# A decoder layer on one core: the mixer's first projection runs ahead of its norm, four residuals one by one, and another pace for the adaLN columns

## The chip, the cores and the metric

The kernel runs on one core of one Trainium2 chip. A core has TensorE (matrix products, PE in the profile, with its weight loads as PEld), VectorE (DVE), ScalarE (ACT), GpSimd (POOL) and SyncE (SP), which here issues the transfers. Each engine works through its own list of instructions in order; semaphores between the lists make one wait for another. The metric is the device time of one execution in microseconds; lower is better.

## The reference

One layer, batch 1, T = 256 tokens, D = 2048, all in float32:

```
mod = silu(c) @ ada_w + ada_b          # 9 vectors of 2048: sh1 sc1 gt1 sh2 sc2 gt2 sh3 sc3 gt3
h = rmsnorm(x) * g1 * (1 + sc1) + sh1
x = x + 0.5 * gt1 * ((silu(h @ wg1) * (h @ wu1)) @ wd1)        # SwiGLU_1, inner width 5632
h = rmsnorm(x) * g2 * (1 + sc2) + sh2
x = x + gt2 * (mixer(h) @ w_out)                               # 8 FoX heads, 8 GatedDeltaNet heads
h = rmsnorm(x) * g3 * (1 + sc3) + sh3
x = x + 0.5 * gt3 * ((silu(h @ wg2) * (h @ wu2)) @ wd2)        # SwiGLU_2
out = rmsnorm(x) * final_norm
```

The mixer projects h onto queries, keys and values of both groups of heads, onto 24 gate columns (forget gate, decay, beta) and onto z. The delta-rule heads put a causal convolution of 4 taps and a SiLU behind their projections, and work in chunks of 64 tokens; the FoX heads do softmax attention with a forgetting term.

## The kernel before, in words

**Layout.** Activations stand transposed: x is 16 tiles of 128 features by 256 tokens. All weights come as one stream of 5392 tiles of 128x128, 8 to a block of 512 KB, 674 blocks in the order of use. A product of float32 values is made from three products of a high part and a low part. So each block is loaded (raw, L124), ACT writes its high part whi (L127), DVE the rest wlo = wraw - whi (L139), and TensorE does three times 256 columns per tile, or 512 and 256 columns where one instruction takes both parts of the activation. Raw, whi and wlo have four buffers each: DVE and ACT can be up to four blocks ahead of TensorE, and a block's wlo has to be there before the third product of its first tile. h is kept as high and low part in hs.

**Stages and blocks.** SwiGLU_1 takes blocks 0 to 263. Its first 28 inner tiles come first (gate and up products to block 111, in pieces over k because the first norm's shift and scale come in bit by bit; partial sums are added up by DVE in acc, L587), then the down product to 167, then 16 inner tiles (gate, up to 231, down to 263). The mixer has 264 to 409: a first projection with four sums at once (24 gate columns and the keys of GatedDeltaNet heads 0 to 2; 64 tiles, 264 to 271), further projections one by one, and the output projection from 378 on: first four columns at once (378 to 385), then 12 columns one by one, two blocks each. SwiGLU_2 has the rest.

**adaLN columns.** mod has 144 columns of 128 values. A column is a transfer of 1 MB (L260) and one reduction of 128x2048 on DVE (L264). The table RATE says, by block, how many columns are issued per block: ada_col is called from Stream.next when the sum passes one. ada_need issues on the spot what is missing.

**Residual and norm.** When a down column is done, residual adds both halves of its sum to x (L516, L517), and sumsq_add squares it on ACT and adds it up on GpSimd (L313, L317). Ahead of the mixer, modulate waits for the last column: norm_sums adds over the features with TensorE (nsum), ACT and DVE make the inverse root, norm_row spreads it over a row with TensorE (nrow), and only then modulate_one writes hs[j] (DVE, ACT, DVE for each of 16 tiles). h_need keeps it four tiles ahead of the products. Ahead of SwiGLU_2 there is another way, class Early: y writes x*g unnormed into hs as soon as a column of x is there, the products start on that, step puts nsum at k = 2 and nrow at k = 4 between them and from then on lets modulate_one overwrite the hs tiles already used, and scaled multiplies the sums by the row afterwards. The shift rides along as two more columns of the moving tile (258 for 256).

**Order.** The program is written once, and a scheduler then orders each engine's list by its own estimates. Inside the mixer, tick counts time along the projections; the generators gates, decays, keys, solve, gdn, fox and to_out are advanced when their last yielded gap has passed. The output projection calls after for the first four columns together, right behind their products; for later columns it waits in the list owed, until tile 8 (LATER) of the next column.

Of the kernel before, what the change touches and what calls it, by code (L numbers as in the profile page):

```python
# [8 lines left out]
F32 = mybir.dt.float32  # L9
# [7 lines left out]
P = 128  # L17
# [10 lines left out]
NH = 8  # L28
# [7 lines left out]
RATE = ((0, 0.5), (12, 0.45), (68, 0.06), (112, 0.5), (168, 0.38), (264, 0.0), (284, 0.26), (404, 0.0), (424, 0.125))  # L36
# [7 lines left out]
LATER = 8  # L44
BEHIND = 2
# [108 lines left out]
def layer_kernel(ctx: ExitStack, tc: tile.TileContext, xrow, c, adaw, cols, cst, w, out, order, dbg=None):  # L154
# [204 lines left out]
    plain = hsf[:, : KD * HS].rearrange("p (k i) -> p k i", k=KD)[:, :, : 2 * T].rearrange("p k (q t) -> p k q t", q=2)  # L359

# [7 lines left out]
    def modulate_one(j, g1, sh, r, weave=True):  # L368

        t = pt("ht")  # L370
        hl, hh, tt = (run(j, LO), run(j, HI), turns(t)) if weave else (plain[:, j, LO], plain[:, j, HI], t)
# [20 lines left out]
    def modulate(which, m_sh, m_sc):  # L392
        ada_need(max(m_sh, m_sc), KD - 1)
        g1 = gains(which, m_sc, 0, KD)
        r = norm_row(norm_sums())
        hq["next"], hq["one"] = 0, lambda j: modulate_one(
            j, g1[:, j : j + 1], mod[:, m_sh * KD + j : m_sh * KD + j + 1], r, False)

    class Early:
# [3 lines left out]
        def __init__(self, which, m_sh, m_sc):  # L403
            self.which, self.m_sh, self.m_sc, self.row, self.rstd = which, m_sh, m_sc, None, None

        def y(self, j):
# [8 lines left out]
            A.activation(run(j, HI), turns(x[:, j]), AF.Copy, scale=g)  # L415
            V.scalar_tensor_tensor(run(j, LO), turns(x[:, j]), g, run(j, HI).bitcast(F32), ALU.mult, ALU.subtract)

        def step(self, k):
# [3 lines left out]
            if k == 4:  # L422
                self.row = norm_row(self.rstd, A.copy)
                g1 = gains(self.which, self.m_sc, 0, KD)
                hq["next"], hq["one"] = 0, lambda j: modulate_one(
                    j, g1[:, j : j + 1], mod[:, self.m_sh * KD + j : self.m_sh * KD + j + 1], self.row)
# [8 lines left out]
        def scaled(self, dst, ps):  # L435
# [4 lines left out]
            V.tensor_tensor(dst, ps[:, :T], self.row, ALU.mult)  # L440
# [308 lines left out]
    norm2 = Early(2, 6, 7)  # L749
# [5 lines left out]
    def mixer():  # L755
        modulate(1, 3, 4)
# [29 lines left out]
        def project(items):  # L786

            pp = [psn(i, "pp") for i in range(len(items))]
            todo = [(i, k) for k in range(KD) for i in range(len(items))]
            for i, k in todo:  # L790
                m, n = items[i]
                h_need(k)
                wh, wl = W.next(m, k, n)
                hh, hl = woven(plain[:, k, HI]), woven(plain[:, k, LO])
# [3 lines left out]
                tick(TILE_US)  # L798
            return [p_[:, :T] for p_ in pp]

        def project_rows(mat, grp):

            pv = [psb("pv0"), psb("pv1")]
            for k in range(KD):
                wh, wl = W.next(mat, k, 4 * grp, 4)
                for t in range(2):
                    hh, hl = (plain[:, k, q, t * P : (t + 1) * P] for q in (HI, LO))
# [17 lines left out]
        def gates(ps):  # L825

            yr = x[:, 8]
            A.copy(runs(yr[R]), turns(ps[R]))
# [93 lines left out]
        def decays(half):  # L922
# [9 lines left out]
            yield 1.0  # L932
# [8 lines left out]
        def conv_silu(ps, n, dst):  # L941
# [4 lines left out]
            for s in range(1, 4):  # L946
                V.scalar_tensor_tensor(cv[:, s:], cp[:, : T - s], tap(3 - s), cv[:, s:], ALU.mult, ALU.add)
# [221 lines left out]
        def fox(h, qk, vt):  # L1169
# [5 lines left out]
            yield 1.0  # L1175
# [14 lines left out]
            yield 3.0  # L1190
# [5 lines left out]
            yield 1.0  # L1196
# [15 lines left out]
            yield 5.0  # L1212
# [8 lines left out]
        def have_keys(h, ps):  # L1221
            kk[h] = otile("kk")
            conv_silu(ps, NH + h, kk[h].bitcast(F32)[:, 0])
# [49 lines left out]
        first = project([("gt", 0)] + [("qkv", NH + h) for h in range(3)])  # L1273
        start("k", -1, gates(first[0]))
        for h in range(3):
            have_keys(h, first[1 + h])
# [6 lines left out]
        for js in [list(range(4))] + [[j] for j in range(4, KD)]:  # L1283

            j = js[0]
            one_ = psf if j < 6 or j >= KD - 2 else pss if j < 8 else psb
            pj = [psn(i, "po") for i in range(len(js))] if len(js) > 1 else [one_("po")]
            if js[0] in BACK:
                x_back(1 + BACK.index(js[0]))
            for i, k in enumerate(ko):  # L1290
# [4 lines left out]
                if owed and i == LATER:  # L1295
                    owed.pop(0)()
# [4 lines left out]
            def after(js=js, pj=pj):  # L1301
# [169 lines left out]
```

## Time and profile before

Three runs: median 1944.64 us, 1944.19 to 1946.02. The profiled execution took 1944.91 us; its span, on which all later times count from zero, is 1943.1 us.

| stretch of the span, us | what runs | PE busy, us | DVE busy, us | granted clock |
|---|---|---|---|---|
| 20.00 to 170.00 | SwiGLU_1, first gate and up pieces | 140.90 of 150.00 | 139.97 | 1.00 |
| 170.00 to 330.00 | its later pieces | 160.00 of 160.00 | 135.65 | 0.99 |
| 330.00 to 483.00 | first down product | 150.90 of 153.00 | 144.28 | 1.00 |
| 483.00 to 740.40 | second gate, up and down | 256.79 of 257.40 | 234.39 | 1.00 |
| 740.40 to 746.60 | to the mixer's first product | 2.29 of 6.20 | 5.50 | 0.70 |
| 769.60 to 1167.00 | mixer behind its first projection | 387.83 of 397.40 | 335.80 | 1.00 |
| 1167.00 to 1184.00 | output projection, around column 5 | 14.30 of 17.00 | 15.80 | 0.90 |
| 1240.00 to 1943.00 | SwiGLU_2 and the end | 694.80 of 703.00 | 461.23 | 1.00 |

How to read it: an engine's row counts time in which at least one of its instructions is under way, so neighbours that overlap by a little (DVE starts the next 128x1024 subtraction 1.13 us after one that took 1.22 us) fill the time without a gap. The clock is the share of full speed that the throttle granted to TensorE. A row of the timeline has start, time from the first start to the last end, engine, line, operation, tiles, count and, in brackets, the idle time of the engine before it and what ended it.

### The profile page before, as it was taken

Reading aid. Unit: us, or ns where it says so; the run is one execution under the profiler, and the core shown is the slowest. Engines: PE = TensorE matmul, PEld = TensorE weight load, DVE = VectorE, ACT = ScalarE, POOL = GpSimd, SP = SyncE. Lnnn points to the kernel's source line nnn. Section 1 sums busy time; section 2 is a strip of 40 time slices with the busy share of each in tenths; the row PEclk is TensorE's granted clock in tenths of the full one; section 3 lists DMA queues with packets and bytes.
Section 4 is the critical chain, followed back from the end, with each engine's and each line's share of the span. In section 5 each row is a group of like instructions: output and inputs, shape, how many; then the busy total and the mean of one; then the engine's idle time right before and its main releaser. Section 6 shows DMA issues by size and latency. Waiting matters only on the chain.

```text
span 1943.1 us, 33703 instructions
## 1 busy us (share of the span) xinstructions
PE 1903.0 (98%) x13086; PEld 1774.5 (91%) x13087; DVE 1555.1 (80%) x2414; ACT 1039.5 (53%) x1647; POOL 57.4 (3%) x55
## 2 busy tenths in 40 slices
PE   8999999999999999999999999999999999999998
PEld 7999999988999988889989998999999999999997
DVE  6999888989999997789987989877676765666654
ACT  7433555433455446857757655665554445555553
POOL 0000000000000020000000002100000000000011
PEclk9999999999999999999999999999999999999999
DMA  9998867999989985596567567677777766666663
GB/s 374 350 344 345 294 215 265 400 374 376 361 347 348 349 307 211 197 330 219 204 254 250 207 229 281 206 246 264 240 246 262 244 231 199 203 199 202 200 201 120
DMA packets 129490, 519.58 MB, mean 267 GB/s; under 512 B 18217, under 2 KB 21545, under 8 KB 111153
## 3 DMA queue, kind: packets, MB, share of 16 engines
q1 hardware_dynamic: 129330, 517.42, 74.1%
q8 instruction: 103, 1.69, 0.3%
q14 instruction: 57, 0.47, 0.1%
HBM read 512.89 MB, written 4.47 MB: 266 GB/s over the span
## 4 chain that ended last, share of the span: by engine, by line
PE 77%; DVE 12%; issue 4%; ACT 3%; DMA 2%; SPq 0%; DVEq 0%; ACTq 0%
PE pd L492 12%; PE pu L488 10%; PE pg L488 10%; PE pd L493 6%; PE pu L489 5%; PE pg L489 5%; DVE wlo L139 5%; PE pgu L574 4%; PE pgu L572 4%; PE pgu L573 4%; DVE adat L264 3%; PE po L492 2%; PE pp L795 2%; PE pp L796 2%; PE pp L797 2%
## 5 line engine op out<-in xcount | busy, mean ns | idle before, releaser
L139 DVE TENSOR_TENSOR wlo<-wraw,whi 128x1024 fp32r<-128x1024 f32 x674 | 820.8, 1225 | 263.8 <-ACT whi L127 262.6
L127 ACT CAST whi<-wraw 128x1024 fp32r<-128x1024 f32 x674 | 698.3, 1045 | 509.4 <-PE pd L492 178.1
L492 PE MATMUL pd<-hid,whi 128*128 128x512 f32 x1408 | 462.1, 382 | 0.0
L493 PE MATMUL pd<-hid,wlo 128*128 128x256 f32 x1408 | 384.8, 274 | 2.7 <-DVE wlo L139 2.7
L264 DVE CUSTOM_DVE_ANT_0 adat<-adat,cs,colt 128x2048 f32<-128x2048 f32 x142 | 334.6, 2357 | 7.6 <-DMA adat<-in_ada_dram 7.4
L488 PE MATMUL pg<-hs,whi 128*128 128x512 f32 x912 | 302.1, 382 | 0.5 <-DVE shc L439 0.5
L488 PE MATMUL pu<-hs,whi 128*128 128x512 f32 x912 | 302.2, 382 | 0.0
L492 PEld LDWEIGHTS pd<-hid,whi 128*128 128x128 f32 x1408 | 266.0, 189 | 36.7 <-DVE hid L507 0.2
L493 PEld LDWEIGHTS pd<-hid,wlo 128*128 128x128 f32 x1408 | 270.2, 192 | 6.0 <-DVE wlo L139 5.6
L489 PE MATMUL pu<-hs,wlo 128*128 128x256 f32 x912 | 249.3, 273 | 0.0
L574 PE MATMUL pgu<-hs,wlo 128*128 128x256 f32 x896 | 240.7, 278 | 8.3 <-DVE wlo L139 8.0
L489 PE MATMUL pg<-hs,wlo 128*128 128x256 f32 x912 | 248.8, 273 | 0.0
L572 PE MATMUL pgu<-hs,whi 128*128 128x256 f32 x896 | 244.8, 276 | 0.8 <-DVE acc L587 0.5
L573 PE MATMUL pgu<-hs,whi 128*128 128x256 f32 x896 | 244.5, 276 | 0.0
L488 PEld LDWEIGHTS pg<-hs,whi 128*128 128x128 f32 x912 | 172.4, 189 | 24.9 <-ACT shc L438 0.7
L488 PEld LDWEIGHTS pu<-hs,whi 128*128 128x128 f32 x912 | 172.4, 189 | 23.6
L795 PE MATMUL pp<-hs,whi 128*128 128x256 f32 x656 | 188.4, 288 | 1.1 <-ACT hs L379 1.1
L797 PE MATMUL pp<-hs,wlo 128*128 128x256 f32 x656 | 182.2, 278 | 0.0
L796 PE MATMUL pp<-hs,whi 128*128 128x256 f32 x656 | 181.9, 277 | 0.0
L574 PEld LDWEIGHTS pgu<-hs,wlo 128*128 128x128 f32 x896 | 168.8, 193 | 11.0 <-DVE wlo L139 10.8
L489 PEld LDWEIGHTS pu<-hs,wlo 128*128 128x128 f32 x912 | 175.0, 192 | 1.4 <-DVE wlo L139 1.4
L489 PEld LDWEIGHTS pg<-hs,wlo 128*128 128x128 f32 x912 | 175.1, 192 | 0.3
(335 smaller groups left out, 2585.9 us busy)
## 6 DMA issues: line engine op xcount, KB each, us to landing
wraw<-in_w_dram SPq DMA_DIRECT2D x674, 512.0 KB, 4.4
adat<-in_ada_dram SPq DMA_DIRECT2D x142, 1024.0 KB, 7.5
xr<-in_xr_dram SPq DMA_DIRECT2D x4, 512.0 KB, 5.6
adaf<-in_ada_dram SPq DMA_DIRECT2D x4, 512.0 KB, 8.5
xd<-x SPq DMA_DIRECT2D x4, 512.0 KB, 6.9
rw<-rowd SPq DMA_DIRECT2D x16, 128.0 KB, 4.2
x<-xd SPq DMA_DIRECT2D x4, 512.0 KB, 5.6
out_dram<-o SPq DMA_DIRECT2D x8, 256.0 KB, 2.6
```

Source lines behind the costliest of these rows:

```text
L127: self.cast = self.nc.scalar.copy(self.h, r).ins
L139: lo_ = nc.vector.tensor_tensor(self.l, r, self.h.bitcast(F32), ALU.subtract)
L264: V.tensor_tensor_reduce(t, t, cs, 1.0, L("adab", q, 1), ALU.mult, ALU.add, mod[:, q : q + 1])
L488: PE.matmul(ps, wt[0], both, start=(k == 0), stop=False)
L489: PE.matmul(ps[:, T:], wt[1], part(k, HI), start=False, stop=(k == KD - 1))
L492: PE.matmul(ps, wt[0], act.rearrange("p q (a b) -> p q b a", a=2), start=first, stop=False)
L493: PE.matmul(ps[:, :T], wt[1], woven(act[:, 0]), start=False, stop=last)
L572: PE.matmul(o, wh, part(k, HI), start=first and s == 0, stop=False, skip_group_check=skip)
L573: PE.matmul(o, wh, part(k, LO), start=False, stop=False, skip_group_check=skip)
L574: PE.matmul(o, wl, part(k, HI), start=False, stop=last, skip_group_check=skip)
L795: PE.matmul(pp[i][:, :T], wh, hh, start=(k == 0), stop=False)
L797: PE.matmul(pp[i][:, :T], wl, hh, start=False, stop=(k == KD - 1))
```

## The change

Seven edits go together.

1. RATE has other steps. Counted with the table alone, the columns issued by blocks 12, 28, 49, 66, 112, 168, 232 and 264 were 8, 15, 24, 32, 35, 63, 88 and 100, and are 8, 16, 25, 32, 41, 69, 96 and 103; from 376 to 424 there are none (before: none from 404). The low steps now lie at 28 to 33, 49 to 56, 66 to 112 and 232 to 264.
2. The mixer uses Early for its first projection. norm1.y is called in the last down product of SwiGLU_1 behind each column's residual; project(..., norm1) starts on the unnormed tiles; the sums go to the buffers 3, 4, 5 and 0 and not 0 to 3.
3. hs has one layout, with the two halves of the tokens apart (stride 144); the plain one, the argument weave and modulate go.
4. gates and the first three conv_silu get their input through scaled (DVE, times the row) and an ACT instruction with the shift as bias, where ACT alone copied it.
5. The four first output columns are owed one by one, and taken at tiles 3 and 11 of the following columns (SLOTS).
6. The yields of decays and fox are longer.
7. conv_silu's loop variable has another name.

```diff
-RATE = ((0, 0.5), (12, 0.45), (68, 0.06), (112, 0.5), (168, 0.38), (264, 0.0), (284, 0.26), (404, 0.0), (424, 0.125))
+RATE = ((0, 0.5), (28, 0.25), (33, 0.5), (49, 0.25), (56, 0.5), (66, 0.2), (112, 0.5), (168, 0.42), (232, 0.24), (264, 0.0), (288, 0.285), (376, 0.0), (424, 0.16))
...
+SLOTS = (3, 11)
...
-    def modulate(which, m_sh, m_sc):
-        ada_need(max(m_sh, m_sc), KD - 1)
-        g1 = gains(which, m_sc, 0, KD)
-        r = norm_row(norm_sums())
-        hq["next"], hq["one"] = 0, lambda j: modulate_one(
-            j, g1[:, j : j + 1], mod[:, m_sh * KD + j : m_sh * KD + j + 1], r, False)
...
-            A.activation(run(j, HI), turns(x[:, j]), AF.Copy, scale=g)
-            V.scalar_tensor_tensor(run(j, LO), turns(x[:, j]), g, run(j, HI).bitcast(F32), ALU.mult, ALU.subtract)
+            A.activation(run(j, HI), self.view(x[:, j]), AF.Copy, scale=g)
+            V.scalar_tensor_tensor(run(j, LO), self.view(x[:, j]), g, run(j, HI).bitcast(F32), ALU.mult, ALU.subtract)
...
-            V.tensor_tensor(dst, ps[:, :T], self.row, ALU.mult)
+            if self.view is turns:
+                V.tensor_tensor(dst, ps[:, :T], self.row, ALU.mult)
+            else:
+                V.tensor_tensor(runs(dst), turns(ps[:, :T]), runs(self.row), ALU.mult)
...
-                        if which == 1:
+                        if which == 0:
+                            norm1.y(j)
+                        else:
...
-    norm2 = Early(2, 6, 7)
+    norm1, norm2 = Early(1, 3, 4, runs), Early(2, 6, 7, turns)
...
-        modulate(1, 3, 4)
...
-        def project(items):
+        def project(items, early=None):
 
-            pp = [psn(i, "pp") for i in range(len(items))]
+            pp = [psn(i if early is None else (3, 4, 5, 0)[i], "pp") for i in range(len(items))]
             todo = [(i, k) for k in range(KD) for i in range(len(items))]
             for i, k in todo:
                 m, n = items[i]
+                if early is not None:
+                    if i == 0:
+                        early.step(k)
+                    early.products(pp[i], W.next(m, k, n), k)
+                    continue
...
+            if early is not None:
+                h_upto(KD)
+                return pp
...
-            A.copy(runs(yr[R]), turns(ps[R]))
+            d = pt("ey")
+            s = norm1.scaled(d, ps)
+            A.activation(yr[R], d[R], AF.Identity, bias=s[R])
...
-            yield 1.0
+            yield 3.0
...
-            A.copy(runs(cp), turns(ps))
+            if early is None:
+                A.copy(runs(cp), turns(ps))
+            else:
+                s = early.scaled(cp, ps)
+                A.activation(cp, cp, AF.Identity, bias=s)
...
-            yield 3.0
+            yield 4.5
...
-            yield 5.0
+            yield 6.5
...
-                if owed and i == LATER:
+                if owed and i in slots:
                     owed.pop(0)()
...
-            if j == 3 or j == KD - 1:
-                after()
-            else:
-                owed.append(after)
+            owed += [lambda j=j, ps=ps: after(j, ps) for j, ps in zip(js, pj)]
+        while owed:
+            owed.pop(0)()
```

What this does to the order shows at three places. The first is TensorE between SwiGLU_1's last down product (pd) and the mixer's first projection (pp). Before:

```order
L493 MATMUL pd<-hid,wlo 128x256
L327 MATMUL nsum<-colt,sqacc 128x2 x2
L327 MATMUL nsum<-colt,sq 128x2 x2
L346 MATMUL nrow<-colt,rb 128x128 x2
L795 MATMUL pp<-hs,whi 128x256 x4
```

Now (the products of k = 0 and 1 stand at the first cut, those of k = 2, 3 and one of k = 4 at the second):

```order
L489 MATMUL pd<-hid,wlo 128x256
L424 MATMUL pp<-hs,whi 128x258
...
L328 MATMUL nsum<-colt,sqacc 128x2 x2
L328 MATMUL nsum<-colt,sq 128x2 x2
L424 MATMUL pp<-hs,whi 128x258
...
L347 MATMUL nrow<-colt,rb 128x128 x2
L424 MATMUL pp<-hs,whi 128x258
```

The projection has moved ahead of both sums of the norm: 24 products stand before nsum and 27 between nsum and nrow.

The second place is DVE behind the first projection, up to the sum that the gates need (pcol, transposed by TensorE from the 24 gate rows; cv is the convolution, cp its input). Before:

```order
L832 TENSOR_SCALAR coef<-coef 128x24
L139 TENSOR_TENSOR wlo<-wraw,whi 128x1024
L947 SCALAR_TENSOR_TENSOR cv<-cp,colt,cv 128x255 x2
L947 SCALAR_TENSOR_TENSOR cv<-cp,colt,cv 128x254 x2
L947 SCALAR_TENSOR_TENSOR cv<-cp,colt,cv 128x253 x2
L839 TENSOR_TENSOR x<-pcol,colt 128x48
```

Now (ey is the gate rows times the norm row):

```order
L958 SCALAR_TENSOR_TENSOR cv<-cp,colt,cv 128x255
L436 TENSOR_TENSOR ey<-pp,nrow 128x256
L958 SCALAR_TENSOR_TENSOR cv<-cp,colt,cv 128x254
L140 TENSOR_TENSOR wlo<-wraw,whi 128x1024
L958 SCALAR_TENSOR_TENSOR cv<-cp,colt,cv 128x253
L846 TENSOR_TENSOR x<-pcol,colt 128x48
```

Before, no DVE instruction stood between the projection and the gate rows; now ey is one of DVE's, and it stands behind the other three sums (cp) and seven of the nine convolution steps of heads 0 to 2. TensorE had pcol 9 tiles behind the first projection; now it has it 29 tiles behind it (at block 275.6).

The third place is DVE behind the four output columns (po; x is the residual, hs the unnormed tile, g its gain). Before:

```order
L139 TENSOR_TENSOR wlo<-wraw,whi 128x1024
L516 SCALAR_TENSOR_TENSOR x<-po,mod,x 128x256 x2
L517 SCALAR_TENSOR_TENSOR x<-po,mod,x 128x256 x2
L516 SCALAR_TENSOR_TENSOR x<-po,mod,x 128x256 x2
L416 SCALAR_TENSOR_TENSOR hs<-x,g_13645,hs 128x2x128
...
L264 ISA adat,mod<-adat,cs,colt 128x2048
...
L139 TENSOR_TENSOR wlo<-wraw,whi 128x1024
L517 SCALAR_TENSOR_TENSOR x<-po,mod,x 128x256
```

Now:

```order
L140 TENSOR_TENSOR wlo<-wraw,whi 128x1024
L512 SCALAR_TENSOR_TENSOR x<-po,mod,x 128x256 x2
L513 SCALAR_TENSOR_TENSOR x<-po,mod,x 128x256 x2
L512 SCALAR_TENSOR_TENSOR x<-po,mod,x 128x256
L140 TENSOR_TENSOR wlo<-wraw,whi 128x1024
L409 SCALAR_TENSOR_TENSOR hs<-x,g_13753,hs 128x2x128
```

Between the subtraction of block 388 and that of 389 stood 17 instructions, a column reduction among them (counted as one); now there are five. To the next two subtractions it is then six and four, and no column stands before block 407.

In SwiGLU_1 the columns at blocks 49 and 54 have moved to 48 and 51 (the one at 48 now follows that block's subtraction), and between 12 and 28 there are eight where there were seven.

More of the change, by code (lines that the diff above doesn't have):

```diff
@@ L425, in step @@
                 hq["next"], hq["one"] = 0, lambda j: modulate_one(
[L426 removed]
+                    j, g1[:, j : j + 1], mod[:, self.m_sh * KD + j : self.m_sh * KD + j + 1], self.row, self.view)
             if k > 4:
@@ L1272, in mixer @@
         W.late = True
-        first = project([("gt", 0)] + [("qkv", NH + h) for h in range(3)])
+        first = project([("gt", 0)] + [("qkv", NH + h) for h in range(3)], norm1)
         start("k", -1, gates(first[0]))
         for h in range(3):
-            have_keys(h, first[1 + h])
+            have_keys(h, first[1 + h], norm1)
         for name in ORDER:
```

40 lines of the change are left out of this document (20 added, 20 removed).

## The prediction

> **What bounds the kernel now.** I read the page's busy times and chain first, then TensorE's waits, then the stretches around the longest waits.
>
> ```profile
> PE 1903.0 (98%) x13086; PEld 1774.5 (91%) x13087; DVE 1555.1 (80%) x2414; ACT 1039.5 (53%) x1647; POOL 57.4 (3%) x55
> PE 77%; DVE 12%; issue 4%; ACT 3%; DMA 2%; SPq 0%; DVEq 0%; ACTq 0%
> ```
>
> TensorE is busy for 98%, so no edit that leaves its products alone can take away much: the 40 us in which it stands, and what a slow clock adds, are all there is. The chain says whom it waits for: DVE above all. TensorE's waits by stretch (line, whom it waited for, total, times, longest; the first row is from 20 to 230 us, the next three from 736 to 760, then two from 760 to 1165 and two from there on):
>
> ```profile
> PE pgu L574 <- DVE wlo L139: 8.0, 10, 2.3
> PE nrow L346 <- DVE rb L345: 1.5, 1, 1.5
> PE nsum L327 <- ACT sq L313: 1.3, 1, 1.3
> PE pp L795 <- ACT hs L379: 1.1, 1, 1.1
> PE pkk L963 <- ACT kk L967: 3.3, 2, 2.2
> PE pft L1215 <- issue: 1.6, 1, 1.6
> PE po L493 <- DVE wlo L139: 2.0, 1, 2.0
> PE po L492 <- ACT whi L127: 0.7, 1, 0.7
> ```
>
> Each is a place that the change touches. What a wait costs beyond itself shows in the windows (microseconds, PE, PEld, DVE, ACT, POOL busy with instruction counts, granted clock, DMA share, GB/s):
>
> ```profile
> 170.00:207.00 37.00, 37.00 (x321) 37.00 (x320) 36.88 (x42) 15.12 (x17) 0.00 (x0) 0.96 0.96 371
> 746.60:749.80 3.20, 3.20 (x15) 3.20 (x16) 3.20 (x9) 2.15 (x6) 0.42 (x2) 0.51 0.48 160
> 749.80:769.60 19.80, 19.80 (x179) 19.80 (x179) 17.47 (x30) 14.69 (x26) 0.00 (x0) 1.00 0.48 158
> 1167.00:1184.00 17.00, 14.30 (x76) 12.37 (x75) 15.80 (x24) 9.18 (x16) 5.50 (x4) 0.90 0.62 237
> ```
>
> At full clock a 256-column product takes 19.80 / 179 = 0.111 us, a tile 0.332, a block of eight tiles 2.65. Behind the norm the clock is 0.51, and 15 products run where 29 would have.
>
> **The norm leaves the path (edit 2).**
>
> ```profile
> 740.24 0.27 PE L493 MATMUL pd<-hid,wlo 128*128 128x256 f32 x1
> 740.35 0.51 PE L327 MATMUL nsum<-colt,sqacc 128*128 128x2 f32 x4
> 742.12 0.61 PE L327 MATMUL nsum<-colt,sq 128*128 128x2 f32 x4 [1.27 <-ACT sq L313]
> 744.25 1.22 PE L346 MATMUL nrow<-colt,rb 128*128 128x128 f32 x4 [1.53 <-DVE rb L345]
> 746.59 1.01 PE L795 MATMUL pp<-hs,whi 128*128 128x256 f32 x3 [1.11 <-ACT hs L379]
> ```
>
> From the last down product to the first of the projection it is 6.35 us, where 0.11 would do: 6.2 lost. Now 24 products (2.65 us) stand ahead of nsum and 27 (3.0) ahead of nrow. The last square ended some 1.8 us behind the last down product, so nsum finds it there; from the square's sum to rb it took 2 us, so nrow does too. What stays are the small products at full clock, about 1.0. The slow clock goes: 14 products at 0.11, 1.5 us. The two shift columns cost 128 products x 2 columns, 0.1. Sum: 6.2 - 1.0 + 1.5 - 0.1 = 6.6 us gained. Bounds: all 7.7, or nothing where something new waits (next part).
>
> What is late next: DVE and the gates. In the order, ey stands behind everything that DVE does from the row on. Durations, starts being closer by what neighbours overlap:
>
> ```profile
> L139 DVE TENSOR_TENSOR wlo<-wraw,whi 128x1024 fp32r<-128x1024 f32 x674 | 820.8, 1225 | 263.8 <-ACT whi L127 262.6
> L372 DVE SCALAR_TENSOR_TENSOR ht<-x,g,nrow 128x256 f32<-128x256 f32 x48 | 21.8, 478 | 0.4
> L500 DVE TENSOR_TENSOR tg<-pg,mg 128x256 f32<-128x256 f32 x57 | 23.8, 418 | 1.1 <-ACT mg L499 1.1
> L379 ACT ACTIVATE hs<-ht,mod 128x256 fp32r<-128x256 f32 x27 | 13.8, 525 | 29.0 <-DVE mod L264 16.6 <-DVE ht L372 11.7 <-PE pu L433 0.6
> 745.51 1.26 DVE L372 SCALAR_TENSOR_TENSOR ht<-x,g,nrow 128x256 f32<-128x256 f32 x3
> ```
>
> Three ht in 1.26 us, the last taking 0.48, are 0.39 apart; by the same 0.09 less, a two-operand step is 0.33 and a subtraction 1.13 apart. From the row to ey: 16 ht 6.2, 16 hs (half with three operands, half with two) 5.8, eight subtractions (blocks 270 to 277) 9.0, seven cv (the kind of ht) 2.7, three cp and ey 1.3, four steps of one value a row 0.5: 25.5 us. The row is there at 2.125 blocks x 2.65 + 1.0 + 0.4 (ACT's copy) = 7.0 us behind the last down product, ey at 32.5, with ACT's bias (0.52) and handing over 33.2. TensorE reaches pcol after 11.625 blocks, 30.8 + 1.0 = 31.8: it waits 1.4. Behind it, the 25 small DVE steps for decay and beta now stand in one run, with two table loads of ACT between them, and TensorE has them only 3.1 blocks later: I take 0.6 more. Together 2.0 lost; from nothing (DVE ahead by 2 us) to 5 (both waits, and a slow stretch of clock as above).
>
> **The extra work in SwiGLU_1's last down product (edit 2).** Per output column DVE gets one more three-operand instruction and a gain. Nearest rows: the same instruction in the output projection (min, median, max in ns), and the two parts of the stretch where it goes:
>
> ```profile
> L416 DVE SCALAR_TENSOR_TENSOR hs<-x,g,hs x16: 478/959/1005, 1171.5 to 1238.1; 128x256 fp32r<-128x256 f32 x16
> 655.00:726.00 71.00, 70.43 (x425) 63.65 (x424) 68.59 (x87) 32.92 (x43) 16.64 (x11) 1.00 0.87 325
> 726.00:740.40 14.40, 14.40 (x91) 13.24 (x90) 8.54 (x13) 7.21 (x9) 2.87 (x3) 1.00 0.89 323
> L317 POOL TENSOR_TENSOR sqacc<-sqacc,sq x42: 731/1118/2787, 669.0 to 1925.3; 128x256 f32<-128x256 f32 x42
> ```
>
> 16 x (0.96 + 0.14 for the gain, whose row stands in the next part) = 17.6 us. DVE is idle for 2.4 + 5.9 = 8.3 there, and RATE frees some 4.5 columns (0.38 to 0.24 over the 32 blocks, none issued in the last columns) at 2.35, 10.6. So it fits by 1.3, and I cost it at nothing; bounds 0 and 2 us, since DVE runs behind first and catches up in the last four columns, where the four buffers cover. The minimum of 478 falls where GpSimd does nothing yet, the median beside its additions: they cost each step 0.48. [...]
>
> **The output projection (edits 1 and 5).**
>
> ```profile
> 1168.02 1.23 DVE L139 TENSOR_TENSOR wlo<-wraw,whi 128x1024 fp32r<-128x1024 f32 x1 [2.70 <-ACT whi L127]
> 1178.25 0.14 DVE L389 SCALAR_TENSOR_TENSOR g<-mod,colt 128x1 f32<-128x1 f32 x1
> 1178.32 1.21 DVE L139 TENSOR_TENSOR wlo<-wraw,whi 128x1024 fp32r<-128x1024 f32 x1
> 1179.59 0.38 PE L493 MATMUL po<-oh,wlo 128*128 128x256 f32 x1 [2.01 <-DVE wlo L139]
> ```
>
> The burst of four residuals and a column keeps DVE from block 389's subtraction for 10.3 us. Now five instructions at 0.39 stand between: it ends 1168.0 + 1.1 + 2.0 + 1.2 = 1172.3, needed 2.0 + 0.7 and three products before 1179.6, about 1176.5. The next three, with six, four and three instructions of 0.07 to 0.87 between, come out some 2 us ahead of need. So 2.0 + 0.7 go, and the slow clock behind them: 17 x (1 - 0.90) = 1.7. Gain 4.4; bounds 2 and 5. The columns go to SwiGLU_2, where DVE is idle a third of the time, and to blocks 66 to 112 and 168 to 232:
>
> ```profile
> 207.00:330.00 123.00, 123.00 (x1103) 123.00 (x1103) 98.77 (x157) 66.83 (x98) 0.00 (x0) 1.00 0.71 238
> 1240.00:1943.00 703.00, 694.80 (x4335) 640.51 (x4334) 461.23 (x616) 351.44 (x499) 17.95 (x14) 1.00 0.65 217
> ```
>
> Six more columns, 14 us, lie beside 24 idle ones; nothing is costed.
>
> [...]
>
> **SwiGLU_1's first pieces (edit 1).**
>
> ```profile
> 105.62 0.38 PE L574 MATMUL pgu<-hs,wlo 128*128 128x256 f32 x1 [2.25 <-DVE wlo L139]
> 157.31 0.69 DVE L587 TENSOR_TENSOR acc<-pgu,acc 128x512 f32<-128x512 f32 x1 [2.19 <-PE pgu L574]
> 157.92 1.22 DVE L139 TENSOR_TENSOR wlo<-wraw,whi 128x1024 fp32r<-128x1024 f32 x1
> 162.91 2.34 DVE L264 CUSTOM_DVE_ANT_0 adat<-adat,cs,colt 128x2048 f32<-128x2048 f32 x1
> 166.98 3.48 DVE L139 TENSOR_TENSOR wlo<-wraw,whi 128x1024 fp32r<-128x1024 f32 x3
> 168.25 0.38 PE L574 MATMUL pgu<-hs,wlo 128*128 128x256 f32 x1 [2.25 <-DVE wlo L139]
> ```
>
> At 157.31 DVE, idle for 2.19, starts on the pieces' sums; block 50's subtraction follows only at 166.98, and TensorE waits 2.25. In the new order block 48's subtraction and an hs step (1.13 + 0.34) stand ahead of that start, so the wait is 0.8, and the clock loss behind it (0.04 x 37 = 1.5) goes: 2.9. The wait at 105.62 stays, its column is still at block 27. Before it DVE has a column more (2.3 us, of which 0.6 is idle now): 1.7 lost. As blocks 28 to 48 then have no more columns than before and TensorE is later, the remaining 0.8 goes as well. Net 2.0 gained; bounds 4.5 gained, 2.5 lost.
>
> **The mixer's gaps (edit 6).** 4.9 us of waits for pkk and pft hang on how ACT's table loads and TensorE's list fall; longer gaps help pft. The ends are all of it with 1.7 of slow clock behind one of them gone (6.6 gained), and 2 lost to new collisions. Since the order still has four keys close together behind ACT's Exp loads, it is nearer to no change: I take 1.0 gained. The strided read of hs is nothing: L574 reads the strided layout already, at the pace of the page's other 256-column products.
>
> **Sum.** 6.6 - 2.0 + 4.4 + 2.0 + 1.0 = 12.0 gained against 1944.9 of the profiled execution (0.3 above the median): 1932.9.
>
> **Rivals.** (a) The mixer's waits go too and the gates do not wait: 1.0 becomes 5, 2.0 becomes 0, so 1926.9. For it: longer gaps. Against: the four keys as before. Chance 0.15. (b) The gates take back all that the norm gave: 6.6, so 1937.5. For it: ey last of four; against: DVE's start must be 4 us later than I have it. 0.13. (c) The change does not do what it says in SwiGLU_1 and the output projection: the waits move on to the next subtraction (columns are the same in number). Only the norm's 4.6 stays with up to 1.5 of the others, or 2.5 are lost in the first pieces: 1939 to 1943. 0.10. (d) Slower: DVE has no room for the y steps. If neither freed columns nor idle time took them, 17.6 us would come on top, 1950.5; it decides from 12 us, two thirds of it, on. For it: 68.59 busy of 71.00. Against: the 10.6 of columns that leave this very stretch. 0.07. (e) GpSimd's addition holds each y step off for its whole 1.12 us: 16 x 0.64 = 10.2 more, 8.9 above the room of 1.3: 1941.8. For it: nothing but the collision itself; against: the maximum of 1005, 0.53 above the minimum. 0.04. [...] My forecast, 1929 to 1937, has the remaining 0.51.
>
> Within 0.2% (3.9 us, about what a measurement of this kernel can tell from no change) lie half of (c) and (e). So faster 0.51 + 0.15 + 0.13 + 0.05 = 0.84, same 0.09, slower 0.07. The range goes from the lower bounds of the mixer and the gates to (c): 1925 to 1942.
>
> **What would show it.** Right: the first projection 0.1 us behind the last down product at clock 1.00; no TensorE wait at blocks 389 to 392; a wait at pcol of 1 to 2 us; a wait near 105 us still there, that near 168 shorter. Wrong: TensorE waits for wlo between 655 and 740 us, a gate wait over 4 us, or as much waiting in 20 to 170 as before.

## The result: 0.3% slower, and the profile after

| | median, us | range of the runs, us | profiled execution, us |
|---|---|---|---|
| before | 1944.9 | 1943.7 to 1946.0 | 1944.9 |
| after | 1950.8 | 1948.9 to 1954.0 | 1951.1 |

The ratio is 1.0032, with an interval of 1.0023 to 1.0041. The forecast was 1932.9 us, with a range of 1925 to 1942. The page of the kernel after has, in its first part and as the shares of the chain:

```profile
PE 1906.4 (98%) x13086; PEld 1777.7 (91%) x13087; DVE 1569.0 (81%) x2455; ACT 1051.7 (54%) x1670; POOL 52.3 (3%) x55
PE 73%; DVE 13%; issue 5%; DMA 5%; ACT 2%; SPq 0%; DVEq 0%; ACTq 0%
```

DVE's share of the chain has grown from 12 to 13%, and that of transfers from 2 to 5%: something now waits for data. TensorE's waits in the kernel after (line, whom it waited for, total, times, longest), the first row from 20 to 230 us, then two from 255 to 350 and four from 760 to 1172:

```profile
PE pgu L570 <- DVE wlo L140: 7.2, 8, 2.7
PE pgu L570 <- DVE wlo L140: 6.0, 5, 1.8
PE pd L489 <- DVE wlo L140: 1.5, 1, 1.5
PE ppt L1204 <- ACT x L1199: 2.7, 1, 2.7
PE pkk L974 <- ACT kk L978: 2.4, 1, 2.4
PE pcol L844 <- ACT x L835: 1.6, 1, 1.6
PE pp L799 <- DVE wlo L140: 1.6, 2, 1.1
```

The second and third rows are new: 7.5 us of waits for subtractions in SwiGLU_1's later pieces and at the head of its first down product, where TensorE did not wait before. The row for the first fox head (ppt) is new too; it was 0.2 us before. Of the kernel after, the stretches that answer to those of before (columns as before: us, PE, PEld, DVE, ACT, POOL busy, granted clock, DMA share, GB/s):

```profile
255.00:350.00 95.00, 87.47 (x752) 85.70 (x752) 78.01 (x125) 48.03 (x72) 0.00 (x0) 1.00 0.72 261
665.00:750.00 85.00, 84.57 (x518) 77.53 (x517) 82.07 (x124) 47.88 (x70) 15.58 (x16) 1.00 0.83 286
749.74:757.74 8.00, 8.00 (x74) 8.00 (x73) 5.66 (x13) 4.31 (x7) 1.32 (x5) 1.00 0.90 302
784.50:790.50 6.00, 6.00 (x39) 5.97 (x40) 4.17 (x14) 5.91 (x9) 0.00 (x0) 0.72 0.55 178
876.30:886.30 10.00, 9.12 (x50) 8.41 (x51) 8.18 (x11) 9.16 (x24) 0.00 (x0) 0.66 0.75 257
1167.00:1184.00 17.00, 17.00 (x109) 15.74 (x108) 14.05 (x33) 9.52 (x17) 1.21 (x1) 1.00 0.84 294
```

The norm's place (third row) and the output projection (last row) run through at full clock (1.00), as forecast. In the first row TensorE stands for 7.5 of 95 us, while DVE is busy for 78 of them only. Rows four and five are slow clock (0.72 and 0.66) behind the waits for pcol (1.6 us) and ppt (2.7 us).

**Where the time went.** For each block the traces show when TensorE first uses its wlo. The table gives how much later (+) or earlier (-) than in the profiled execution of before that is, in us, with the first block of both set to zero; it holds the experiments too. So it leaves out what differs ahead of block 0: e3 and e12 reach that block 2.0 and 2.1 us later than before, the others within 0.5 us of it.

| kernel | 66 | 112 | 232 | 263 | 272 | 288 | 320 | 378 | 392 | last |
|---|---|---|---|---|---|---|---|---|---|---|
| after | -0.8 | +8.2 | +10.5 | +9.5 | +3.5 | +7.0 | +12.1 | +12.4 | +6.4 | +6.3 |
| e1_rate_low_66_112 | -1.0 | -0.7 | +0.7 | -1.0 | -7.1 | -3.9 | -0.4 | +1.2 | -4.8 | -4.9 |
| e2_reduce_later | -0.9 | -0.9 | +5.7 | +4.8 | -1.3 | +0.7 | +4.4 | +4.6 | -1.3 | -1.4 |
| e3_before_new_rate | -0.9 | +7.0 | +9.3 | +7.6 | +8.6 | +5.6 | +6.1 | +6.3 | -0.1 | +0.1 |
| e4_old_gaps | -2.5 | +6.8 | +9.1 | +8.1 | +2.1 | +6.0 | +6.4 | +7.0 | +0.4 | +0.2 |
| e5_rate_and_old_gaps | -2.5 | -2.5 | -1.1 | -2.8 | -8.9 | -7.1 | -7.4 | -5.6 | -12.2 | -11.1 |
| e6_after_old_rate | 0.0 | 0.0 | 0.0 | +5.9 | -0.2 | +1.0 | +0.3 | +0.4 | -4.0 | -1.6 |
| e7_gates_later | -0.9 | -0.9 | +0.5 | -1.2 | -7.2 | -10.2 | -6.2 | -4.3 | -10.2 | -8.8 |
| e8_before_one_by_one | 0.0 | +0.6 | +0.6 | +0.7 | +1.7 | -0.5 | -1.0 | -1.0 | -1.5 | -0.3 |
| e9_late_old_gaps | -2.5 | -2.5 | -0.6 | -2.2 | -8.3 | -4.8 | -4.6 | -5.5 | -12.2 | -12.4 |
| e12_late_new_gaps | -0.9 | -0.9 | +1.0 | -0.6 | -6.7 | -6.4 | -3.5 | -4.6 | -10.5 | -10.7 |
| e10_late_old_gaps_gates_later | -1.1 | -1.1 | +0.8 | -0.8 | -6.9 | -5.6 | -6.2 | -6.9 | -13.6 | -13.7 |
| e13_late_new_gaps_gates_later | -0.9 | -0.9 | +1.0 | -0.7 | -6.7 | -8.0 | -6.5 | -6.6 | -12.5 | -12.7 |

In the kernel after, 9.0 us are lost from block 66 to 112 and 2.3 more up to 232; then 1.0 is gained up to 263, 6.0 gained at the norm (263 to 272), 3.5 lost at the gates (to 288), 5.4 lost in the mixer (to 378, nearly all by 320), and 6.0 gained in the output projection (378 to 392).

**What stands in blocks 66 to 112.** DVE's waits for the transfer of a column, in the kernel after from 255 to 350 us:

```profile
DVE adat L265 <- DMA adat<-in_ada_dram: 14.3, 6, 3.5
```

The same wait in the kernel before, from 207 to 330 us:

```profile
DVE adat L264 <- DMA adat<-in_ada_dram: 2.6, 1, 2.6
```

One of them in the timeline of the kernel after, with rows of SP's queue, DVE and TensorE:

```profile
273.73 0.43 SPq L261 DMA_DIRECT2D adat<-in_ada_dram  x1
...
273.91 1.22 DVE L140 TENSOR_TENSOR wlo<-wraw,whi 128x1024 fp32r<-128x1024 f32 x1
...
276.90 1.23 DVE L140 TENSOR_TENSOR wlo<-wraw,whi 128x1024 fp32r<-128x1024 f32 x1 [0.52 <-ACT whi L128]
281.59 2.35 DVE L265 CUSTOM_DVE_ANT_0 adat<-adat,cs,colt 128x2048 f32<-128x2048 f32 x1 [3.46 <-DMA adat<-in_ada_dram]
...
284.54 1.21 DVE L140 TENSOR_TENSOR wlo<-wraw,whi 128x1024 fp32r<-128x1024 f32 x1
...
285.80 0.38 PE L570 MATMUL pgu<-hs,wlo 128*128 128x256 f32 x1 [1.77 <-DVE wlo L140]
```

SP issues the column at 273.73. DVE is through with what stands ahead of the reduction some 4.4 us later, at 278.1, and stands until 281.59. The next subtraction is late, and TensorE waits for it. From issue to landing the columns of this stretch took 5.5 to 7.8 us (the tile's summary; in the kernel before the median of the same window was 6.6):

```profile
DMA to landing us min/median/max: 5.5/7.5/7.8
```

The lists tell why DVE comes too soon. In SP's list a column's transfer stands behind the load of its block. In SwiGLU_1 its reduction mostly stands in DVE's list right behind the subtraction of the same block, and SP is up to four blocks ahead. But for the nine columns issued in blocks 66 to 112 the scheduler put the reduction 0, 1, 2, 2, 3, 3, 3, 3 and 3 subtractions earlier than that, so most of the four blocks of lead are gone. In the kernel before, the three columns at blocks 81, 98 and 112 stand 3 subtractions earlier as well; they waited 2.6, 0.1 and 0.1 us, and TensorE never for them. With nine, one every five blocks, DVE's slack no longer covers the waits, and TensorE has the 7.5 us of the rows above.

### The profile page after: what moved, and what is told of

Its sections match the earlier page's. It is cut to its first block, busy times and chain, and to the rows that moved or that the text cites. A ratio compares the mean times of both kernels' runs of the same rounds, so it can differ in the third digit from the quotient of the medians.

```text
span 1949.1 us, 33807 instructions
## 1 busy us (share of the span) xinstructions
PE 1906.4 (98%) x13086; PEld 1777.7 (91%) x13087; DVE 1569.0 (81%) x2455; ACT 1051.7 (54%) x1670; POOL 52.3 (3%) x55
## 4 chain that ended last, share of the span: by engine, by line
PE 73%; DVE 13%; issue 5%; DMA 5%; ACT 2%; SPq 0%; DVEq 0%; ACTq 0%
PE pd L488 14%; PE pu L484 10%; PE pg L484 10%; PE pd L489 7%; PE pu L485 5%; PE pg L485 5%; DVE wlo L140 5%; PE po L488 3%; DVE adat L265 3%; DMA adat<-in_ada_dram 3%; PE pgu L570 2%; PE pgu L568 2%; PE pgu L569 2%; PE pp L799 2%; PE pp L797 2%
## 5 line engine op out<-in xcount | busy, mean ns | idle before, releaser
L570 PE MATMUL pgu<-hs,wlo 128*128 128x256 f32 x896 | 240.8, 279 | 13.6 <-DVE wlo L140 13.1
L568 PEld LDWEIGHTS pgu<-hs,whi 128*128 128x128 f32 x896 | 172.6, 193 | 1.1 <-ACT whi L128 0.5
L797 PE MATMUL pp<-hs,whi 128*128 128x256 f32 x592 | 172.5, 291 | 0.4 <-ACT whi L128 0.4
L569 PEld LDWEIGHTS pgu<-hs,whi 128*128 128x128 f32 x896 | 172.6, 193 | 0.3 <-DVE hs L382 0.3
```

The costliest lines, as they stand in the source:

```text
L568: PE.matmul(o, wh, part(k, HI), start=first and s == 0, stop=False, skip_group_check=skip)
L569: PE.matmul(o, wh, part(k, LO), start=False, stop=False, skip_group_check=skip)
L570: PE.matmul(o, wl, part(k, HI), start=False, stop=last, skip_group_check=skip)
L797: PE.matmul(pp[i][:, :T], wh, hh, start=(k == 0), stop=False)
```

## The experiments

Ratios are to the kernel before, run beside each experiment on the same chip. They come in three sets (e1 to e4, e5 to e8, the rest); medians are compared within a set.

**e1: few columns in blocks 66 to 112.** Of the kernel after:

```diff
-... (66, 0.2), ... (288, 0.285), ...
+... (66, 0.06), ... (288, 0.355), ...
```

> The changed kernel with 0.06 in place of 0.20 in RATE's step from block 66 to 112; the six columns go to the mixer's step from 288 to 376 (0.355 in place of 0.285). Both theories of the loss in blocks 84 to 112 (late transfers, or the six columns' DVE work) expect TensorE's waits there to go and block 112 to come 8 to 9 us earlier than in the changed kernel. At the end: 8 to 9 us faster (1942) if the mixer takes six more columns (14 us of DVE) beside its idle time; about no change (1950) if it gives them back.

Measured: 1940.1 us, ratio 0.9974 (0.9964 to 0.9984). Block 112 comes 8.9 us earlier than in the kernel after (+8.2 to -0.7), as expected. It is faster than before by 4 us, and 2 us faster than the 1942 expected. The six columns were not quite free in the mixer: from 760 to 900 us there are four waits for subtractions, where the kernel after has two of 1.6 us together:

```profile
PE pp L799 <- DVE wlo L140: 3.7, 4, 1.4
```

**e2: the same columns, reduced later.** The reduction is put two blocks behind its transfer's block, in blocks 66 to 111:

```diff
+        late = W.late or 66 <= len(W.order) // WB < 112
+
         def total():
-            with nullcontext() if W.late else W.behind(False):
+            with nullcontext() if late else W.behind(False):
...
-        if W.late:
+        if late:
             W.owing.append((len(W.order) // WB, total))
...
-        W.settle()
+        if m or len(W.order) // WB < 66:
+            W.settle()
```

> The changed kernel with the same columns at the same blocks, but in blocks 66 to 111 a column's reduction is put two blocks behind the block at which its transfer is issued; in the changed kernel it stands up to three subtractions ahead of that block in DVE's list. DVE's work is the same. Theory 1, DVE stands in its list waiting for transfers that were issued too late: block 112 comes 7 to 9 us earlier, time about 1942. Rival, the 14 us of added DVE work itself delays the subtractions: no change, 1949 to 1951.

Measured: 1944.4 us, ratio 0.9998 (0.9989 to 1.0008). DVE has the same work, and block 112 comes 9.1 us earlier (+8.2 to -0.9). What is left of DVE's wait from 252 to 342 us, and, from the timeline, a column's issue and its reduction 18.6 us later:

```profile
DVE adat L267 <- DMA adat<-in_ada_dram: 0.4, 1, 0.4
```

```profile
257.30 0.43 SPq L261 DMA_DIRECT2D adat<-in_ada_dram  x1
...
275.90 2.34 DVE L267 CUSTOM_DVE_ANT_0 adat<-adat,cs,colt 128x2048 f32<-128x2048 f32 x1
```

So the work of the added columns is not the cause of the loss up to block 112; the late transfer is. Behind block 112 the last late reduction and the first usual one fall on neighbouring subtractions: 2.3 us of wait and a clock of 0.79 over the next 8 us cost 4.2 us by block 130. That is a flaw of this edit.

**e3: the new RATE alone, in the kernel before.**

```diff
-RATE = ((0, 0.5), (12, 0.45), (68, 0.06), ...
+RATE = ((0, 0.5), (28, 0.25), (33, 0.5), (49, 0.25), (56, 0.5), (66, 0.2), ...
```

> The kernel before with the new RATE alone. If the loss in blocks 84 to 112 belongs to RATE and to nothing else: 9 us lost at block 112 against the kernel before, 1 gained in the first pieces, 1 to 3 gained in the output projection (no column left there, four residuals still in one run), so 4 to 7 us slower than before, 1949 to 1952. If the other edits have a part in it: within 2 us of the kernel before.

Measured: 1947.1 us, ratio 1.0011 (0.9999 to 1.0023). It loses 7.9 us from block 66 to 112, with none of the other edits there. In the output projection it gains 6.4 us, all that the kernel after gains, with the four residuals still in one run; I had expected 1 to 3. The time lies between the two answers (1949 to 1952; within 2 us of before): the loss came as the first says, and the gain behind it was larger.

**e4: the old yields** (1.0, 3.0, 1.0, 5.0 in fox and 1.0 in decays) in the kernel after:

```diff
-            yield 3.0
+            yield 1.0
...
-            yield 4.5
+            yield 3.0
...
-            yield 6.5
+            yield 5.0
```

> The changed kernel with the old yields in fox and decays (1.0, 3.0, 1.0, 5.0 and 1.0). If the longer gaps make the wait of 2.8 us for the first fox head's transposed tile at 876 us and the slow clock behind it: the 5 us lost in blocks 302 to 306 go, 1945 to 1947. If that loss comes from the gates and keys being later by edit 2, whatever the gaps are: no change, 1949 to 1952.

Measured: 1946.0 us, ratio 1.0006 (0.9996 to 1.0015). Blocks 288 to 320 cost 0.4 us where the kernel after loses 5.1.

**e5: the edits of e1 and e4 together, in the kernel after.**

> The changed kernel with both the RATE of e1_rate_low_66_112 and the old yields of e4_old_gaps. If the longer yields cost 3 to 5 us in blocks 288 to 310 whatever comes ahead of them: 3 to 5 us faster than e1_rate_low_66_112, 1935 to 1937. If the gain of e4_old_gaps hung on how that one run's instructions fell: 1939 to 1942.

Measured: 1939.0 us, ratio 0.9962 (0.9950 to 0.9974). That is the lower end of the second answer (1939 to 1942); by the ratios it is 2.3 us faster than e1, where the first answer asked for 3 to 5. The intervals of e1 and e5 overlap, and e5's profiled execution (1934.1) was its fastest, so the table flatters it. The pair alone does not settle the yields.

**e6: the old RATE in the kernel after.**

```diff
-RATE = ((0, 0.5), (28, 0.25), (33, 0.5), (49, 0.25), (56, 0.5), (66, 0.2), ...
+RATE = ((0, 0.5), (12, 0.45), (68, 0.06), ...
```

> The changed kernel with the RATE of before, edit 1 undone alone. Three places tell. Block 112: 8 to 9 us earlier than in the changed kernel (few columns in blocks 66 to 112). Blocks 232 to 263: if the work of y fits only because the new RATE lowers the columns there (17.6 us of it, 8.3 idle), 5 to 9 us are lost there; if it fits anyhow, none. Output projection: if four residuals one by one are enough, blocks 386 to 392 stay as in the changed kernel; if the missing column was it (the kernel before with the new RATE alone had the whole gain), 2 to 5 us are lost there. Sum: 1942 if it fits and the residuals are enough, 1951 to 1956 if neither.

Measured: 1944.2 us, ratio 0.9996 (0.9987 to 1.0005). Up to block 232 it runs as the kernel before. Then 5.9 us are lost in blocks 232 to 263; TensorE's waits from 655 to 745 us are

```profile
PE pd L489 <- DVE wlo L140: 3.0, 4, 0.9
PE pd L489 <- DVE gh L510: 2.4, 3, 0.8
```

So y's work fits only with the new RATE's lower step there. The time is neither of the two sums (1942; 1951 to 1956), since y did not fit and most of the output projection's gain came all the same. In blocks 288 to 320 nothing is lost, although the yields are the new ones. In the output projection it gains 4.4 us by block 392, and gives 2.4 of it back in the next output columns, up to block 402.

**e7: gates later, in e1.**

```diff
             V.tensor_scalar(coef, coef, -1.0, None, ALU.mult)
-            yield 2.0
+            yield 12.0
```

> e1_rate_low_66_112 with the first yield of gates 12.0 in place of 2.0: pcol stands 1.1 blocks (3 us) later in TensorE's list, prow 2.4 and the keys' products 4 blocks later. If pcol waits because DVE comes to ey last and its place is too early: the wait of 1.8 us and the slow clock behind it go, 3 us gained by block 279 and kept, 1937. If the wait only moves to prow, to the keys (pkk waits 2.3 us there) or to the first row of the solver: gained by 279 and lost by block 310, 1939 to 1942.

Measured: 1939.4 us, ratio 0.9967 (0.9954 to 0.9980). The wait for pcol is gone; from block 272 to 288 TensorE gains 3.0 us where e1 loses 3.2. Between blocks 288 and 320 it loses 4.0, but e1 loses 3.5 there as well. A new wait of 4.1 us for a query (qv) is among it. The profiled executions say 3.9 us gained at the end, the ratios 1.4 us with overlapping intervals; the median is in the second answer (1939 to 1942), so this pair does not show that the gain is kept.

**e8: residuals one by one (edit 5 alone), in the kernel before.**

```diff
+            slots = SLOTS if len(owed) > 1 else (LATER,)
...
-                if owed and i == LATER:
+                if owed and i in slots:
...
+            owed += [lambda j=j, ps=ps: after(j, ps) for j, ps in zip(js, pj)]
+        while owed:
+            owed.pop(0)()
```

> The kernel before with edit 5 alone: the four residuals one by one at tiles 3 and 11, with the old RATE. If one by one is enough for the waits at blocks 386 to 392: 4 to 5 us faster than before, 1939 to 1941. If the column that fell among them was the cause: no change, 1943 to 1945.

Measured: 1945.1 us, ratio 1.0003 (0.9993 to 1.0012): no change. From 1140 to 1240 us TensorE waits

```profile
PE pft L1216 <- DVE on L1212: 2.0, 1, 2.0
PE po L494 <- DVE wlo L140: 1.3, 2, 0.9
```

The wait of 2.0 us for block 389's subtraction is gone, but 1.3 us come back at later subtractions, and a fox head's transpose now waits 2.0 us for its input from DVE. Block by block the edit does act: blocks 386 to 390 gain 5.1 us. But blocks 384 to 386, where that transpose stands, lose 4.1, and 2.1 are given back up to block 396. The column that stood among the residuals (its reduction came behind block 388's subtraction) now stands behind block 385's, ahead of the head's last steps on DVE.

**e9, e12, e10, e13: late reductions, with both yields and both places of the gates.** All four have e2's reductions for blocks 66 to 109 and no column from 106 to 111, so that none falls on its neighbour. e9 and e10 have e4's yields too, e10 and e13 e7's gates. Beside e2's diff, with 110 for 112:

```diff
-... (66, 0.2), (112, 0.5), ... (288, 0.285), ...
+... (66, 0.2), (106, 0.0), (112, 0.5), ... (288, 0.3), ...
```

> The changed kernel with three things undone or mended: reductions two blocks behind their transfers in blocks 66 to 109, no column from 106 to 111 (one column fewer, made up from block 288 on with 0.3), and the old yields. The late transfers' 8 to 9 us and, whatever made it, the mixer's 5 us should both be gone: 1936 to 1939.

> As e9_late_old_gaps, but with the new yields. In its list TensorE has the first fox head's ppt at block 305.25, two blocks behind plog; in the changed kernel, with the same yields, it stood at 304.0, 0.75 behind plog. Theory, the place in the list makes the wait of 2.8 us and the slow clock at 876 us: no such wait in blocks 302 to 306, 1936 to 1939. Rival, the longer yields themselves cost it: 4 to 5 us lost in blocks 288 to 310, 1941 to 1944.

> e9_late_old_gaps with the first yield of gates 12.0 in place of 2.0, which puts pcol 1.1 blocks later in TensorE's list. If the 3 to 4 us that this gained by block 279 in e7_gates_later are kept when nothing else is late: 1932 to 1936. If the later keys give them back between 300 and 320, as there: 1936 to 1939.

> e12_late_new_gaps with the first yield of gates 12.0. The same two answers as for e10_late_old_gaps_gates_later: 1932 to 1936 if kept, 1936 to 1939 if given back; and if the yields of fox are of no account, within 2 us of e10_late_old_gaps_gates_later.

| us (ratio, interval) | old yields | new yields |
|---|---|---|
| gates as in the kernel after | e9: 1935.6 (0.9949, 0.9937 to 0.9962) | e12: 1938.1 (0.9961, 0.9948 to 0.9973) |
| gates later | e10: 1929.4 (0.9917, 0.9904 to 0.9931) | e13: 1933.4 (0.9942, 0.9930 to 0.9955) |

All four lose nothing in blocks 66 to 112 and nothing in the 18 blocks behind them, with the new RATE's columns in full but one; between 130 and 232 they lose 1.9. By the medians the gates' later place gains 6.2 and 4.7 us. The table has only 1.3 and 2.0 of that: e9's profiled execution (1932.7) was the fastest of its five, and e10's (1931.4) the slowest. The new yields cost 2.5 and 4.0. Expected were 1936 to 1939 for e9, which came out just below, and 1932 to 1936 or 1936 to 1939 for e10 and e13: e13 is in the first, e10 below both. My theory that ppt's place in TensorE's list makes the first fox head's wait falls: in e12, whose time is where the theory put it (1936 to 1939), ppt stands two blocks behind plog (the logits' product), and still TensorE waits from 840 to 900 us

```profile
PE ppt L1207 <- ACT x L1202: 4.0, 2, 3.9
```

e10 is the fastest kernel of the study, 0.8% faster than before and some 1.1% faster than the changed kernel. Its page:

```profile
PE 1899.5 (98%) x13086; PEld 1773.1 (92%) x13087; DVE 1567.4 (81%) x2455; ACT 1047.0 (54%) x1666; POOL 53.8 (3%) x55
PE 82%; DVE 10%; issue 3%; ACT 3%; DMA 2%; SPq 0%; DVEq 0%; ACTq 0%
```

DVE does what it does in the kernel after (1567 us busy); its share of the chain has fallen from 13 to 10%, and the transfers' from 5 to 2.

## Why the prediction was wrong

| step of the prediction | forecast, us | bounds | measured, us |
|---|---|---|---|
| first pieces (blocks 0 to 66) | -2.0 | -4.5 to +2.5 | -0.8 |
| six columns more (blocks 66 to 112; 112 to 232) | 0 | none given | +9.0; +2.3 |
| y beside the last down product (232 to 263) | 0 | 0 to +2 | -1.0 |
| norm off the path (263 to 272) | -6.6 | -7.7 to 0 | -6.0 |
| gates (272 to 288) | +2.0 | 0 to +5 | +3.5 |
| mixer's gaps (288 to 378) | -1.0 | -6.6 to +2 | +5.4 |
| output projection (378 to 392) | -4.4 | -5 to -2 | -6.0 |

**The step that failed** is the sentence "Six more columns, 14 us, lie beside 24 idle ones; nothing is costed". It counted busy time against idle time in a stretch, and the sum was right: DVE had the room, since e2 does the same work there and loses nothing before block 112. What failed is that idle time of an engine that works in order is not free for any work at any place. The reduction holds the subtractions behind it until its own transfer has landed, and its lead over that transfer was 4.4 us where 7.9 were needed. The kernel before showed the wait once (2.6 us, the row above), in the very window whose busy time the sentence quotes, and the new list has eight of the nine reductions ahead of their own blocks' subtractions. From issue to landing a column of the nine took 7.5 us in the median, beside the weights' loads. Bounds of nothing to 9 x 2.6 us could have been read from the row of that one wait, and would have put both signs into the range.

The same sentence costs the columns that went to blocks 168 to 232 at nothing. From block 112 to 232 the kernels with the new RATE's steps there lose 1.4 to 2.3 us (e2, with the flaw described above, more), and e6, with the old RATE, loses none. What makes this smaller loss is not shown.

Rival (d), "Slower", has 1950.5 us against the 1950.8 measured. That is chance: its mechanism, no room for the y steps, cost nothing in the kernel after.

**The mixer's gaps** are the second miss, outside the bounds too. The part named the right kind of loss (new collisions) and gave it 2 us. What came is one chain at the first fox head. On DVE of the kernel after:

```profile
871.32 1.23 DVE L935 TENSOR_TENSOR Ln<-cstt,x 128x1024 f32<-128x1024 f32 x1 [1.12 <-DMA x<-rowd]
...
875.21 0.43 DVE L914 TENSOR_TENSOR dec<-cstt,rw 128x256 f32<-128x256 f32 x1 [2.11 <-DMA rw<-rowd]
875.55 0.16 DVE L1197 TENSOR_SCALAR fmx<-fmx 128x2 f32<-128x2 f32 x1
```

DVE stands twice for a decay row whose transfer was issued some 4 and 7 us earlier (at 866.8 and 868.3); behind it stands the head's maximum (fmx), on that ACT's exponential, on that ppt. TensorE waits 2.7 us, and the clock is at 0.66 for the next 10, another 3.4. In the kernel after it is the mechanism of blocks 66 to 112 again: a step in order ahead of its data. e4, which differs in the yields alone, bears that out: there DVE stands 2.5 us for the same row at 872.83, but fmx is ahead of it in the list, at 870.20, and ppt waits 0.5 us only.

In all four pairs that differ in the yields alone the new ones were slower: after and e4 by 0.26% of the time before, e1 and e5 by 0.12%, e12 and e9 by 2.5 us, e13 and e10 by 4.0 us. The intervals of e1 and e5 overlap, and so do those of e12 and e9; but in the table, too, the new yields are behind in every pair, by 4.4, 3.6, 2.5 and 2.7 us from block 288 to 378 and by 0.6 to 0.8 in the output projection. So the yields cost some 2 to 5 us. What stays open is how each kernel comes by its share, since the wait for ppt does not go with the yields: e9, with the old ones, waits 3.1 us, and e1 and e13, with the new ones, have no such wait. In e9 and e12 DVE does not stand for a decay row there; ACT stands 1.8 and 2.7 us for a weight block's transfer ahead of the exponential. And e6 has the new yields with the old RATE and loses nothing in these blocks, and e12 waits for ppt longer (3.9 us at once) but loses less, its clock being at 0.83 over the next 10 us.

**The gates** came out at +3.5, inside the bounds. DVE took 25.8 us from its first ht to ey (forecast 25.5); it began some 1.6 us later than forecast, and TensorE came to pcol as much later. TensorE waited 1.6 us for pcol (forecast 1.4), and the clock behind it was 0.72 for 6 us, 1.7 us more. The forecast had put the slow clock into the bound only. e7, e10 and e13 confirm the cause, DVE late and pcol's place too early: moved by 1.1 blocks it no longer waits.

**The norm** did what was forecast: the first projection follows the last down product without a gap,

```profile
749.41 0.27 PE L489 MATMUL pd<-hid,wlo 128*128 128x256 f32 x1
749.52 0.28 PE L424 MATMUL pp<-hs,whi 128*128 128x258 f32 x1
```

and all kernels with the edit gain 6.0 to 6.1 us from block 263 to 272.

**The y work** fits, and for the reason given: the new RATE takes columns out of that stretch. Without (e6) it costs 5.9 us, of the 9.3 that 17.6 us of work against 8.3 idle ones would have left over. So rival (d) was the right mechanism for the old RATE. Rival (e) is out: the y steps took

```profile
L409 DVE SCALAR_TENSOR_TENSOR hs<-x,g,hs 128x256 fp32r<-128x256 f32 x15 | 13.4, 892 | 0.0
```

0.89 us each from 664 to 750 us, no more than the 0.96 that the sum used, against the 1.6 of the rival. Thirteen of the fifteen took 0.95 to 0.97 us and met an addition that, by GpSimd's times (which are rough in a profile), had 0.66 to 0.68 us still to run; held off until its end they would have taken 1.15, with the 0.48 that a step takes alone (the two that met none took 0.48 and 0.47). So these steps were not held off until the addition's end, as rival (e) has it: beside one a step took some 0.48 us more, not 0.67.

**The output projection** gained more than forecast, and edit 5 alone does not explain it. "Five instructions at 0.39 stand between" names the right wait, and one-by-one residuals do remove it: in e8 blocks 386 to 390 gain 5.1 us. But with the old RATE the columns make new waits around it, so that e8 ends where the kernel before does, and e6, with all edits but the first, keeps 2.0 of the 4.4 us it had gained. That is the mechanism of rival (c): the waits move on. e3 shows that RATE alone, which leaves no column's reduction in blocks 376 to 406, gains 6.4 us with the residuals in one run. So either edit removes the wait, and what keeps the gain is edit 1.

**The first pieces** gained 0.8 in some executions and 2.5 in others, with the same waits (next section but one); the forecast lies between.

Every sign that the prediction named came as it should: no gap at the norm, no wait at blocks 389 to 392, pcol at 1.6 us, the wait near 105 us there and that near 168 shorter (1.0), hardly a wait from 655 to 740, less waiting in the first pieces. They all lay where a gain was claimed, and none in a stretch that was costed at nothing.

## What to carry to other kernels

When work is moved into the idle time of an engine that runs in order, count two things and not one: the busy time that it adds, and the lead between the issue of its data and its place in the engine's list, against the time to landing in that stretch. Where a single wait of that kind stands in the trace of before, price it times the number of moved steps, as a bound. And put a sign to look for at every term that was costed at nothing, since those are the ones that nobody checks.

## What had not been expected of the hardware

The same wait at the same place is followed by a slow clock in one execution and not in another. Four windows, the first two of the kernel after, then two of e9, whose lists are the same up to there:

```profile
103.30:106.70 3.40, 0.68 (x7) 0.49 (x5) 3.40 (x6) 1.88 (x3) 0.00 (x0) 1.00 0.20 76
107.00:110.00 3.00, 3.00 (x16) 3.00 (x16) 3.00 (x3) 0.00 (x0) 0.00 (x0) 0.50 0.71 208
```

```profile
103.30:106.70 3.40, 0.68 (x7) 0.49 (x5) 3.40 (x6) 1.88 (x3) 0.00 (x0) 1.00 0.18 66
107.00:110.00 3.00, 3.00 (x29) 3.00 (x29) 3.00 (x3) 1.05 (x1) 0.00 (x0) 1.00 0.67 197
```

Both stand for 2.72 us and run seven products in the first window; then one runs 16 products in 3 us, at a clock of 0.50, and the other 29, at 1.00. From 106.70 to 113.50 us it is 47 products against 61, some 1.6 us, and it is seen in the table as -0.8 or -2.5 at block 66. So here a wait of 2.7 us on TensorE costs either itself or itself and some 1.6 more. That may be one reason why the executions of one kernel scatter by a few us (e5: 1934.1 to 1941.0); no run separates it from others. What decides between the two is not shown.
